# First projection reordered: queries, keys, values; second filters behind the queries; low parts and absolute sums on VectorE

## The chip, the cores and the metric

The kernel runs on one core of one Trainium2 chip. The metric is the device time of one execution in microseconds; of several executions the median is given. TensorE (PE) multiplies, VectorE (DVE), ScalarE (ACT) and GpSimd (POOL) work on elements, SyncE (SP) issues most transfers.

## What is computed

A two-layer backbone over 256 latent tokens of width 1024, with 256 context tokens. Layer 0 mixes by a Hyena long convolution and a neighbourhood attention from one combined projection; layer 1 by a Fourier transform; then a dense SwiGLU and a top-2-of-8 expert SwiGLU. The part around the change, cut from the reference:

```python
h  = modulate(rmsnorm(x, g_mix), sh1, sc1)          # 256 x 1024
z  = h @ w_in                                       # 3072 columns
q, k, v = split(z[..., 1536:], 3)                   # 512 each
hc = modulate(rmsnorm(ctx, g_mix), csh1, csc1)
kc, vc = split(hc @ w_in[:, 2048:], 2)              # context: keys and values only
y_na = neighborhood_attention(q, k, v, kc, vc, rpb)
filt = k / (sum(abs(k), axis=0) + EPS)              # two implicit filters, from a small sine network
y = x1 * long_conv(v_hy, filt[:, 0]);  y = x2 * long_conv(y, filt[:, 1])
x = x + gt1 * (concat([y_hy, y_na]) @ w_mix_out)
```

## The kernel before

All matrices are float32. A projection is made of three multiplications: each operand is split into a high part that the fast float format holds (ScalarE copies it) and a low part (the difference, an elementwise subtraction), and `mm3` (lines 105 to 108) issues high x low, low x high and high x high in turn.

Up to the output projection a scheduler orders the instructions; it takes the program's order as priority and places what it holds to be ready. The queues of PE, VectorE, ScalarE, GpSimd and SyncE each run strictly in the order it wrote.

- `ada_first` (line 117) multiplies the conditioning with the first ada weights, eight pieces of 1 MB (L130), and gives the scales a_x and a_c (line 204).
- `filters(o)` (line 362) makes filter o: four multiplications h2 x fw3 (L367) into psB buffers, each times a decay on VectorE (L369); the absolute values on ScalarE (L373); their sums on GpSimd (L374, L375) into absum; sum and difference of the two sides on VectorE (L377, L378). `spectra(o)` (line 381) multiplies these with a cosine and a sine table (L353) and adds and subtracts the halves (L343 to L348, into kre and kim). L460 adds absum over the partitions.
- `hT_split` (line 219) takes the normalised rows, transposes two 128-column blocks at a time on PE into a psA buffer (L224; there are two psA buffers), scales them into hf (one half on ScalarE, L228, one on VectorE, L229; two hf buffers), copies the high part on ScalarE (L233) and subtracts for the low part (L234). It is called for the latent rows (four pieces, hxh and hxl) and for the context rows (four pieces, hch and hcl). The low part is taken by VectorE, but GpSimd takes the first latent piece and all four context pieces.
- `proj` (line 411) splits 128 columns of the weights (L113 on ScalarE, L114 on VectorE, tiles wsh and wsl, two buffers) and multiplies them into a psA buffer: 24 multiplications for latent rows, 24 more for context rows if `both`. The loop at line 448 goes over six 1 MB pieces of w_in: 8 and 9 are keys, 10 and 11 values, 6 and 7 queries; each has two chunks, keys and values with context rows (48 multiplications), queries without (24). `qkv_chunk` (line 426) moves the result into qT, kT, vb and vc, the values with further transposes (L441, L445).
- `filters(1)` stands ahead of that loop, `spectra(1)` behind it. After the loop the context tiles are given back (`es_hc.close`) and their memory goes to attention.
- `dense` (line 536) lists the Hyena work: twelve chunks of 24 multiplications (`in_step`, z by L473 to L476) and the two convolutions; `issue` mixes them with 32 heads of attention (`Head`, lines 593 to 642): scores (L609 to L615, from qm, which ScalarE copies from qT at L571), maximum (L619), exp (L621), transposes (L626), values (L637, L640). The ada weights of later steps are added up on VectorE (L153).
- From the output projection on, the order is written by hand: the dense SwiGLU, the Fourier layer, the experts.

The lines that the change rewrites:

```python
374        nc.gpsimd.tensor_add(ab[0], ab[0], ab[1])
375        nc.gpsimd.tensor_add(absum[:, o, :], ab[0][:, 0, :], ab[0][:, 1, :])
404    hT_split(np_, xnx, a_x, b_x, hxh, hxl, 0, psA, "a", sub=lambda k: (nc.gpsimd, nc.vector)[k > 0])
407    hT_split(np_, xnc, a_c, b_c, hch, hcl, 0, psA, "a", sub=lambda k: nc.gpsimd)
408    with tc.issue_after(last_mm[0]):
409        filters(1)
448    for n in (8, 9, 10, 11, 6, 7):
452        if n == 7:
453            with tc.issue_after(last_mm[0]):
454                spectra(1)
```

Of the kernel before, what the change touches and what calls it, by code (L numbers as in the profile page):

```python
# [34 lines left out]
def backbone(ctx, tc, x, c, cx, c_ctx, w_ada, b_ada, norm_g, w_in, short_w, short_b,  # L35
# [4 lines left out]
    nc = tc.nc  # L40
# [62 lines left out]
    last_mm = [None]  # L103
# [115 lines left out]
    def hT_split(pool, xn, a, b, hi, lo, off, ps_pool, tag, keep=None, each=None, sub=None):  # L219
        for k2 in range(4):  # L220
            ps = T(ps_pool, [P, 2, 2 * P], tag)
            for kk in range(2):
                for t in range(2):
                    nc.tensor.transpose(ps[:, kk, t * P:(t + 1) * P],  # L224
                                        xn[:, t, (2 * k2 + kk) * P:(2 * k2 + kk + 1) * P], ident)
            hf = keep[:, 2 * k2:2 * k2 + 2, :] if keep is not None else T(pool, [P, 2, 2 * P], "hf", bufs=2)
            k = 2 * k2
            nc.scalar.activation(hf[:, 0, :], ps[:, 0, :], AF.Identity, bias=b[:, k:k + 1], scale=a[:, k:k + 1])  # L228
            nc.vector.tensor_scalar(hf[:, 1, :], ps[:, 1, :], a[:, k + 1:k + 2], b[:, k + 1:k + 2],  # L229
                                    op0=OP.mult, op1=OP.add)  # L230
            if hi is not None:
                hs = hi[:, k:k + 2, off:off + 2 * P]
                nc.scalar.copy(hs, hf)  # L233
                (sub or (lambda k: nc.vector))(k2).tensor_sub(lo[:, k:k + 2, off:off + 2 * P], hf, hs.bitcast(F32))  # L234
            if each is not None:
                each(k2)
# [11 lines left out]
    hxh = T(hx, [P, ND, S], "hxh", F32R)  # L248
# [113 lines left out]
    def filters(o):  # L362
        hr = T(fp, [P, 2, 2, 512], "hr")
        for t in range(2):
            for d in range(2):
                ps = T(psB, [P, 512], "b")
                nc.tensor.matmul(ps, h2[:, t * P:(t + 1) * P],  # L367
                                 fw3[:, (2 * o + d) * 512:(2 * o + d + 1) * 512], start=True, stop=True)
                nc.vector.tensor_mul(hr[:, t, d, :], ps, decay[:, t, :])  # L369
        nc.vector.memset(hr[0:1, 0, 1, :], 0.0)  # L370
        ab = [T(fp, [P, 2, 512], "ab", bufs=2) for _ in range(2)]
        for t in range(2):
            nc.scalar.activation(ab[t], hr[:, t], AF.Abs)  # L373
        nc.gpsimd.tensor_add(ab[0], ab[0], ab[1])  # L374
        nc.gpsimd.tensor_add(absum[:, o, :], ab[0][:, 0, :], ab[0][:, 1, :])  # L375
        hp = T(fp, [P, 2, 512], "ab", bufs=2)
        nc.vector.tensor_add(hp, hr[:, :, 0, :], hr[:, :, 1, :])  # L377
        nc.vector.tensor_sub(hr[:, :, 0, :], hr[:, :, 0, :], hr[:, :, 1, :])  # L378
        fbox[o] = (hp, hr)
# [21 lines left out]
    b_c = modx[:, 0:2, :].rearrange("p a b -> p (a b)")  # L401
    xnx = normalise(np_, x_sb, "nx")
    xnc = normalise(np_, ctx_box[0], "nc", out=ctx_box[0], junk=kim[:, 1].rearrange("p a b -> p (a b)"))
    hT_split(np_, xnx, a_x, b_x, hxh, hxl, 0, psA, "a", sub=lambda k: (nc.gpsimd, nc.vector)[k > 0])
    with tc.issue_after(last_mm[0]):
        spectra(0)
    hT_split(np_, xnc, a_c, b_c, hch, hcl, 0, psA, "a", sub=lambda k: nc.gpsimd)
    with tc.issue_after(last_mm[0]):
        filters(1)

    def proj(w, both, eng=None):
        wh, wl = split(wsp, w, [P, ND, P], "ws", eng=eng)
# [32 lines left out]
                nc.tensor.transpose(tp[:, t, :], vT[:, S + t * P:S + (t + 1) * P], ident)  # L445
            nc.vector.tensor_copy(vc[:, :, cs], tp[:, 0:2, :])

    for n in (8, 9, 10, 11, 6, 7):
        w = win_piece(n)
        for j in range(2):  # L450
            qkv_chunk(w[:, :, j * P:(j + 1) * P], 2 * n + j - 12)
        if n == 7:
            with tc.issue_after(last_mm[0]):
                spectra(1)
    es_hc.close()
    es_f.close()
    psn = T(psS, [P, 8], "s")
# [1272 lines left out]
```

## Time and profile before

| | |
|---|---|
| median of 3 runs | 1470.87 us (1466.68 to 1473.18) |
| profiled execution | 1472.97 us, its span 1471.1 us |
| mean granted clock of TensorE | 0.989 of full speed |
| PE busy | 1412.9 us (96%) |
| DVE, ACT, POOL busy | 587.3, 322.8, 115.5 us |
| HBM read | 465.48 MB, 317 GB/s over the span |

In a timeline row stand the start in us, the length in us, the engine, the line, the operation, the tiles out<-in (buffer numbers left out) with their forms, and how many instructions the row merges; in brackets the idle time of the engine just before it and what ended it. Instructions overlap a little: the price of one in a row of its kind is the distance from start to start.

### The profile page before, as it was taken

What the parts mean: (1) busy time and instruction counts of PE and PEld (TensorE: products, weight loads), DVE (VectorE), ACT (ScalarE), POOL (GpSimd) and SP (SyncE); (2) the same over time, 40 slices, a digit from 0 to 9 for tenths busy, and PEclk for the clock granted to TensorE, in tenths of its full rate; (3) what the DMA queues carried; (4) which work ended last, traced back from release to release, by engine and by line L of the source; (5) the groups of instructions that cost most, each with busy time, mean ns of one, the idle gap of its engine ahead of it and who ended that gap; (6) DMA issues with size and microseconds to landing.
All of it is one profiled execution on the core that took longest, in us unless ns stands there. A gap on an engine that the chain in (4) does not pass through costs nothing.

```text
span 1471.1 us, 23080 instructions
## 1 busy us (share of the span) xinstructions
PE 1412.9 (96%) x9597; PEld 768.6 (52%) x9597; DVE 587.3 (40%) x942; ACT 322.8 (22%) x613; POOL 115.5 (8%) x107
## 2 busy tenths in 40 slices
PE   6999999989999898999999999998999999999997
PEld 1598677779899764334335333333335333333332
DVE  3636888789999763102112110114212111012412
ACT  3425444554444441000001000000101010000001
POOL 1501110023351010000000000000000000000000
PEclk9999999999999999999999999999999999999999
DMA  9435454279999766999999999999899999999895
GB/s 350 135 92 160 158 187 171 87 278 372 330 321 337 260 237 234 367 378 363 387 396 388 395 393 393 394 393 391 317 395 387 394 393 393 394 394 388 316 393 226
DMA packets 205398, 468.42 MB, mean 318 GB/s; under 512 B 8559, under 2 KB 43728, under 8 KB 204168
## 3 DMA queue, kind: packets, MB, share of 16 engines
q1 hardware_dynamic: 202576, 462.03, 85.2%
q0 software_dynamic: 1680, 2.29, 0.7%
q10 hardware_dynamic: 1000, 2.24, 0.5%
q8 instruction: 85, 1.39, 0.4%
q14 instruction: 57, 0.47, 0.1%
HBM read 465.48 MB, written 1.05 MB: 317 GB/s over the span
## 4 chain that ended last, share of the span: by engine, by line
PE 60%; DVE 1%; issue 0%; ACT 0%
PE w L1518 27%; PE y L1550 13%; PE w L1514 9%; PE y L1543 4%; PE w L1531 2%; PE y L1258 1%; PE w L1580 1%; PE w L1258 1%; PE y L1580 1%; PE w L1573 1%; DVE ysb L1560 0%; DVE total L1582 0%; DVE aT L1535 0%; DVE ysb L1562 0%; DVE x L1664 0%
## 5 line engine op out<-in xcount | busy, mean ns | idle before, releaser
L1518 PE MATMUL w<-w,hg 128*64 128x512 f32 x1792 | 401.9, 597 | 2.7 <-issue 2.7
L1518 PEld LDWEIGHTS w<-w,hg 128*64 128x64 f32 x1792 | 124.1, 137 | 241.1 <-issue 237.2
L1550 PE MATMUL y<-w,aT 128*64 128x512 f32 x896 | 200.8, 595 | 1.5 <-DVE aT L1535 1.5
L1522 ACT ACTIVATE a<-w 64x512 f32<-64x512 f32 (+1 forms) x91 | 46.5, 511 | 661.7 <-PE w L1518 451.7
L1523 DVE TENSOR_TENSOR a<-a,w 64x512 f32<-64x512 f32 (+1 forms) x91 | 52.8, 580 | 327.7 <-ACT a L1522 327.7
L1535 DVE COPY aT<-w 128x256 f32<-128x256 f32 (+2 forms) x77 | 31.1, 411 | 311.8 <-PE w L1531 290.9
L1514 PE MATMUL w<-w,hg 128*32 128x256 f32 x2240 | 132.7, 381 | 0.0
L1550 PEld LDWEIGHTS y<-w,aT 128*64 128x64 f32 x896 | 61.9, 137 | 132.6 <-issue 129.8
L1514 PEld LDWEIGHTS w<-w,hg 128*32 128x32 f32 x2240 | 67.0, 109 | 64.1 <-issue 24.2
L106 PE MATMUL f<-hh,wh 128*128 128x256 f32 x344 | 97.3, 283 | 0.8 <-ACT hh L933 0.8
L108 PE MATMUL f<-hh,wl 128*128 128x256 f32 x344 | 96.7, 281 | 0.5 <-DVE wl L114 0.5
L107 PE MATMUL f<-hl,wh 128*128 128x256 f32 x344 | 96.6, 281 | 0.1
L113 ACT CAST wsh<-w 128x1024 fp32r<-128x1024 f32 x57 | 59.4, 1046 | 74.0 <-PE a L107 50.1
L114 DVE TENSOR_TENSOR wl<-w,wh 128x1024 fp32r<-128x1024 f32 x46 | 69.9, 1560 | 6.1 <-ACT wh L113 6.1
L1543 PE MATMUL y<-w,aT 128*32 128x512 f32 x560 | 66.8, 594 | 2.7 <-DVE aT L1535 2.7
L106 PEld LDWEIGHTS f<-hh,wh 128*128 128x128 f32 x344 | 64.8, 188 | 1.9 <-ACT hh L933 1.0
L107 PEld LDWEIGHTS f<-hl,wh 128*128 128x128 f32 x344 | 64.8, 188 | 1.3 <-DVE hl L934 0.3
L108 PEld LDWEIGHTS f<-hh,wl 128*128 128x128 f32 x344 | 64.8, 188 | 0.7 <-DVE wl L114 0.7
L114 DVE TENSOR_TENSOR wsl<-w,wsh 128x1024 fp32r<-128x1024 f32 x39 | 48.5, 1246 | 37.2 <-ACT wsh L113 37.0
L114 POOL TENSOR_TENSOR wsl<-w,wsh 128x1024 fp32r<-128x1024 f32 x18 | 52.1, 2893 | 118.3 <-ACT wsh L113 118.3
L106 PE MATMUL a<-hxh,wsh 128*128 128x256 f32 x192 | 54.9, 286 | 0.9 <-DVE z L476 0.9
L820 DVE SCALAR_TENSOR_TENSOR adacc<-w,colAs,adacc 128x1024 f32<-128x1024 f32 x32 | 55.4, 1733 | 0.3
(441 smaller groups left out, 1835.7 us busy)
## 6 DMA issues: line engine op xcount, KB each, us to landing
w<-in_moe_w_dram SPq DMA_DIRECT2D x336, 1024.0 KB
w<-in_w_ada_dram SPq DMA_DIRECT2D x44, 1024.0 KB
w<-in_ffn_w_dram SPq DMA_DIRECT2D x33, 1024.0 KB
w<-in_w_in_dram SPq DMA_DIRECT2D x12, 1024.0 KB
w<-in_w_mix_out_dram SPq DMA_DIRECT2D x4, 1024.0 KB
w<-in_w_fourier_dram SPq DMA_DIRECT2D x4, 1024.0 KB
s<-in_w_ada_dram SPq DMA_DIRECT2D x2, 1024.0 KB
raw<-in_na_rpb_dram POOLq DMA_DIRECT2D x32, 62.5 KB, 3.0
```

The lines of the kernel that those rows point to most:

```text
L106: nc.tensor.matmul(ps, lh, rh, start=first, stop=False)
L107: nc.tensor.matmul(ps, lh, rl, start=False, stop=False)
L108: last_mm[0] = nc.tensor.matmul(ps, ll, rh, start=False, stop=last).ins
L113: nc.scalar.copy(hi, src)
L114: (eng or nc.vector).tensor_sub(lo, src, hi.bitcast(F32))
L820: nc.vector.scalar_tensor_tensor(st["acc"], w, colA_s[:, k:k + 1], st["acc"], op0=OP.mult, op1=OP.add)
L1514: nc.tensor.matmul(ps[32 * j:32 * j + 32, 0:256], hg[:, k, 0:32], w, start=(k == 0), stop=(k == ND - 1), tile_position=(0, 32 * j))
L1518: nc.tensor.matmul(ps[64 * j:64 * j + 64, :], hg[:, k, 0:64], ws[j][k // 4][:, k % 4, :], start=(k == 0), stop=(k == ND - 1), tile_positio ...
L1522: nc.scalar.activation(a[b3:b3 + 64, 0:n], ps[b1:b1 + 64, 0:n], AF.Silu)
L1523: nc.vector.tensor_mul(a[b3:b3 + 64, 0:n], a[b3:b3 + 64, 0:n], ps[b3:b3 + 64, 0:n])
L1543: nc.tensor.matmul(y[32 * j:32 * j + 32, :], aT[:, f, 32 * q:32 * q + 32], w2[fc // 2][:, fc % 2, h * 512:(h + 1) * 512], start=(first and ...
L1550: nc.tensor.matmul(y[64 * j:64 * j + 64, :], aT[:, f, :], w2[f // 2][:, f % 2, h * 512:(h + 1) * 512], start=(first and f == 0), stop=(las ...
```

## The change

The first projection takes pieces 6 and 7 (queries) first, then 8 and 9 (keys), then 10 and 11 (values). `filters(1)` is called behind the last query chunk instead of ahead of the loop, `spectra(1)` behind the last value chunk. The low parts of all pieces of `hT_split` and the two additions of absolute values are VectorE's.

```diff
@@ filters @@
-        nc.gpsimd.tensor_add(ab[0], ab[0], ab[1])
-        nc.gpsimd.tensor_add(absum[:, o, :], ab[0][:, 0, :], ab[0][:, 1, :])
+        nc.vector.tensor_add(ab[0], ab[0], ab[1])
+        nc.vector.tensor_add(absum[:, o, :], ab[0][:, 0, :], ab[0][:, 1, :])
@@ backbone @@
-    hT_split(np_, xnx, a_x, b_x, hxh, hxl, 0, psA, "a", sub=lambda k: (nc.gpsimd, nc.vector)[k > 0])
+    hT_split(np_, xnx, a_x, b_x, hxh, hxl, 0, psA, "a")
     with tc.issue_after(last_mm[0]):
         spectra(0)
-    hT_split(np_, xnc, a_c, b_c, hch, hcl, 0, psA, "a", sub=lambda k: nc.gpsimd)
-    with tc.issue_after(last_mm[0]):
-        filters(1)
+    hT_split(np_, xnc, a_c, b_c, hch, hcl, 0, psA, "a")
...
-    for n in (8, 9, 10, 11, 6, 7):
+    for n in (6, 7, 8, 9, 10, 11):
         w = win_piece(n)
         for j in range(2):
             qkv_chunk(w[:, :, j * P:(j + 1) * P], 2 * n + j - 12)
-        if n == 7:
+        if n in (7, 11):
             with tc.issue_after(last_mm[0]):
-                spectra(1)
+                (filters if n == 7 else spectra)(1)
```

What the scheduler makes of it, at three places. PE's order around the context transposes (a_367 to a_397 are psA buffers with transposes of the context rows, w_240; b_... are psB buffers of the second filters), before:

```order
L353 MATMUL b_361<-hr_186,dft_113 128x512
L367 MATMUL b_408<-fw_32_140,fh_44_184 128x512
L224 MATMUL a_367<-ident_61,w_240 128x128 x4
L224 MATMUL a_377<-ident_61,w_240 128x128 x4
L367 MATMUL b_411<-fw_32_140,fh_44_184 128x512
L224 MATMUL a_387<-ident_61,w_240 128x128 x4
L367 MATMUL b_414<-fw_32_140,fh_44_184 128x512
L224 MATMUL a_397<-ident_61,w_240 128x128 x4
L367 MATMUL b_417<-fw_32_140,fh_44_184 128x512
L106 MATMUL a_436<-hxh_80,wsh_432 128x256
```

In the changed program the same place, and the place behind the fourth query chunk (a_505), ahead of the first key chunk (a_560):

```order
L353 MATMUL b_361<-hr_186,dft_113 128x512
L224 MATMUL a_367<-ident_61,w_240 128x128 x4
L224 MATMUL a_377<-ident_61,w_240 128x128 x4
L224 MATMUL a_387<-ident_61,w_240 128x128 x4
L224 MATMUL a_397<-ident_61,w_240 128x128 x4
L106 MATMUL a_413<-hxh_80,wsh_409 128x256
...
L108 MATMUL a_505<-hxh_80,wsl_502 128x256
L367 MATMUL b_532<-fw_32_140,fh_44_184 128x512
L367 MATMUL b_535<-fw_32_140,fh_44_184 128x512
L367 MATMUL b_538<-fw_32_140,fh_44_184 128x512
L106 MATMUL a_560<-hxh_80,wsh_556 128x256
```

The four L367 have left the transposes; three stand together behind the queries, the fourth eight multiplications later.

VectorE's order in the changed program from the scaling of the last two latent pieces to that of the third context piece (a_387); what stands ahead of it there are the scalings of the first two latent pieces and the two halves of kre:

```order
L234 TENSOR_TENSOR hxl_81<-hf_316,hxh_80 128x512
L234 TENSOR_TENSOR hxl_81<-hf_326,hxh_80 128x512
L114 TENSOR_TENSOR wsl_410<-w_407,wsh_409 128x1024
L229 TENSOR_SCALAR hf_336<-a_331,a_x_286,mod_8_74 128x256
L229 TENSOR_SCALAR hf_346<-a_341,a_x_286,mod_8_74 128x256
L344 TENSOR_TENSOR kim_118<-sE_359,b_361 128x512
...
L229 TENSOR_SCALAR hf_382<-a_377,a_c_288,modx_76 128x256
L114 TENSOR_TENSOR wsl_440<-w_407,wsh_439 128x1024
L234 TENSOR_TENSOR hcl_285<-hf_372,hch_284 128x512
L234 TENSOR_TENSOR hcl_285<-hf_382,hch_284 128x512
L229 TENSOR_SCALAR hf_392<-a_387,a_c_288,modx_76 128x256
```

Before, hxl of hf_316 and all four hcl were GpSimd's and stood nowhere in this row, the second wsl stood behind the last context piece, and two L369 stood between the scalings of the first three context pieces.

ScalarE's order where attention begins (z of the last Hyena chunks a_1399 and a_1451, qm, the first probabilities pe) in the changed program:

```order
L113 CAST wsh_1447<-w_1393 128x1024
L471 ACTIVATE z_1103<-a_1340,colA_71 128x256
L471 ACTIVATE z_1103<-a_1399,colA_71 128x256
L471 ACTIVATE z_1103<-a_1451,colA_71 128x256
L569 COPY qm_1123<-qT_90 32x128 x8
L619 ACT_TABLE_LOAD
L619 ACTIVATE pe_1277,sums_1133<-s_1271,nm_1134 128x384
```

Before, L571 (now L569) stood behind z of a_1241, the fourth Hyena chunk, and four chunks followed it. On PE the scores of the first head now stand behind the last multiplication of a_1451.

## Rows read from the trace of the kernel before

**Rows 1.** The page's slices: PE's busy tenths in 40 equal slices.
```profile
PE   6999999989999898999999999998999999999997
```
**Rows 2.** PE's timeline from 28 to 66 us.
```profile
40.93 1.05 PE L460 MATMUL s<-ones,absum 128*128 128x1 f32 x8 [0.95 <-POOL absum L375]
...
57.34 1.12 PE L367 MATMUL b<-fw,fh 64*128 64x512 f32 x2
58.39 0.66 PE L224 MATMUL a<-ident,w 128*128 128x128 f32 x4
58.98 1.12 PE L367 MATMUL b<-fw,fh 64*128 64x512 f32 x2
60.03 0.39 PE L106 MATMUL a<-hxh,wsh 128*128 128x256 f32 x1
```
**Rows 3.** PE's timeline: projection chunks at 72 to 84 us, Hyena chunks at 132 us.
```profile
72.31 0.39 PE L108 MATMUL a<-hxh,wsl 128*128 128x256 f32 x1 [0.35 <-DVE wsl L114]
...
77.83 0.28 PE L106 MATMUL a<-hxh,wsh 128*128 128x256 f32 x1
...
83.49 0.28 PE L106 MATMUL a<-hxh,wsh 128*128 128x256 f32 x1
...
132.64 0.35 PE L106 MATMUL a<-hxh,wsh 128*128 128x256 f32 x1 [0.46 <-DVE z L476]
```
**Rows 4.** VectorE's timeline from 38 to 54 us and at 149 us.
```profile
38.52 1.22 DVE L377 TENSOR_TENSOR ab<-hr 128x1024 f32<-128x1024 f32 x1 [2.24 <-POOL ab L374]
...
47.30 0.16 DVE L204 SCALAR_TENSOR_TENSOR a_c<-modx,colA 128x8 f32<-128x8 f32 x1
...
52.25 0.68 DVE L234 TENSOR_TENSOR hxl<-hf,hxh 128x512 fp32r<-128x512 f32 x1
52.85 0.53 DVE L229 TENSOR_SCALAR hf<-a,a_x,mod 128x256 f32<-128x256 f32 x1
53.30 0.67 DVE L344 TENSOR_TENSOR kim<-sE,b 128x512 f32<-128x512 f32 x1
...
149.38 1.28 DVE L153 SCALAR_TENSOR_TENSOR adacc<-w,colAs,adacc 128x1024 f32<-128x1024 f32 x1
```
**Rows 5.** Windows: PE, PEld, DVE, ACT, POOL busy (instructions), granted clock, DMA share, GB/s.
```profile
42.00:44.00 2.00, 2.00 (x12) 0.50 (x16) 0.00 (x0) 0.00 (x0) 0.00 (x0) 0.56 0.05 11
44.00:46.00 2.00, 2.00 (x10) 0.50 (x2) 0.67 (x1) 0.00 (x0) 0.00 (x0) 0.59 0.00 0
...
54.00:56.00 2.00, 1.06 (x6) 0.71 (x6) 2.00 (x4) 1.28 (x3) 0.00 (x0) 1.00 0.00 0
...
188.00:192.00 4.00, 2.64 (x17) 2.12 (x16) 4.00 (x7) 0.78 (x1) 0.00 (x0) 0.63 0.94 291
...
544.00:548.00 4.00, 2.28 (x13) 1.56 (x12) 2.35 (x6) 1.61 (x5) 1.13 (x2) 0.93 0.00 0
548.00:552.00 4.00, 4.00 (x36) 1.53 (x35) 1.13 (x2) 2.28 (x5) 3.19 (x4) 0.65 0.01 4
```
**Rows 6.** GpSimd's timeline at 57 us.
```profile
57.47 1.27 POOL L234 TENSOR_TENSOR hcl<-hf,hch 128x512 fp32r<-128x512 f32 x1 [6.23 <-ACT hch L233]
```
**Rows 7.** ScalarE's timeline from 139 to 146 us.
```profile
139.41 0.56 ACT L473 ACTIVATE z<-a,colA 128x256 f32<-128x256 f32 x1
139.87 2.46 ACT L571 COPY qm<-qT 32x128 f32<-32x128 f32 x8
...
144.61 1.28 ACT L621 ACT_TABLE_LOAD   x1
145.91 0.58 ACT L621 ACTIVATE pe<-s,nm 128x384 f32<-128x384 f32 x1
```
**Rows 8.** PE's timeline from 158 to 192 us.
```profile
158.00 0.59 PE L609 MATMUL s<-kT,qm 128*128 128x256 f32 x2
...
159.31 0.31 PE L637 MATMUL o<-vb,pT 128*64 128x32 f32 x4
...
190.72 0.80 PE L615 MATMUL s<-bias,jrev 128*128 128x128 f32 x2 [1.36 <-DVE bias L602]
```

## The prediction

> **What bounds the kernel now.** I read the slices of the page first. PE stands at 8 or 9 tenths from the second slice to the last [rows 1], so nothing but PE's own chain sets the end: a change pays if it takes a wait or a stretch of low clock out of PE's row, and costs if it puts one in. Everything the change touches lies in the first 210 us. I therefore went to PE's timeline from 28 to 66 us [rows 2], where the normalised rows are transposed and split and the second filters are multiplied. PE waits there for absum from GpSimd (0.95 us before L460) and for ScalarE and VectorE before the L367 multiplications. The first projection multiplication stands at 60.03; from there a chunk of 48 runs through in 5.66 us (77.83 to 83.49), so 24 of them take 2.83 us [rows 3]. VectorE's row shows what paces the transposes: from 48 us on one operation starts where the last ends (52.25, 52.85, 53.30 [rows 4]). Last I read the granted clock by stretch [rows 5]: it fell to half (1.2 GHz) for most of 42 to 46 us after the wait at L460, again in 188 to 192 us and after 544 to 548 us, where PE had been busy for 2.28 of 4 us, but not in 54 to 56 us, where it was busy for 1.06 of 2 us.
>
> **The change part by part.**
>
> *Sums of absolute values on VectorE.* The additions L374 and L375 leave GpSimd. On VectorE they are two additions of the forms that stand in [rows 4], 128x1024 at 1.22 us and 128x512 at 0.68 us, and they fall into the 2.24 us in which VectorE waits for GpSimd's sum ahead of L377. So absum is there before PE reaches L460, and the 0.95 us wait goes. **-0.95 us.**
>
> *First low parts on VectorE.* Five subtractions of 512 elements leave GpSimd, 1.27 us each there [rows 6], and cost VectorE 0.60 us each from start to start [rows 4]. What PE waits for is in the compiled order: the first projection chunk takes the psA buffer that the third context piece leaves, so it starts when VectorE has scaled that piece (L229 on a_387). Ahead of that, counted from a_c at 47.30, VectorE now has six L229 at 0.45, ten operations of 512 elements at 0.60 (kre, kim, six low parts) and two wsl of L377's size, 1.22: 2.7 + 6.0 + 2.4 = 11.1 us, with 0.7 us until its first L229 may start and 0.55 for the L229 itself and the hand-over, 12.4 us. In the kernel before it was 60.03 - 47.46 (end of a_c) = 12.57 us. **-0.2 us.** So VectorE's two added low parts, and one wsl that moved ahead, eat what the four L369 and the memset leave. Bounds: if the buffer did not gate, the last query low part would (four L229, seven of 512, one wsl, the same 0.7: 7.9 us), -4.5 us; if VectorE stands still once for ScalarE, a wsl's length, +1.2 us.
>
> The Trainium skill, "GPSIMD Engine Reference", section Engine selection, would have elementwise additions on VectorE because GpSimd is about twice as slow with two inputs. The rows agree on the price of one (1.27 against 0.68 us); by that rule five of them would bring the start forward by 5 x 0.6 = 3.0 us and the sum would be 2.8 us lower than mine. I don't take it, because here VectorE is the queue and GpSimd was not.
>
> *Second filters behind the queries.* The four L367 cost 1.05 us each from start to start (57.34 to 58.39 [rows 2]). Before, they stood in time in which PE waited for the transposes anyway, so their removal there gains nothing beyond the start above. Now three stand back to back behind the fourth query chunk and one eight multiplications later, in a row that has no waits: 4 x 1.05 = **+4.2 us**, between 3.4 (if a fifth of it is the change of operands, which goes where three stand together) and 4.5 (1.12 us, the length of one). VectorE's part (four L369, memset, the sums, L377, L378: some 8 us) lies beside a K chunk of 5.66 us and the next; wsl for the chunk after stands behind it and is needed only 5.66 us later. The wait of 0.35 us for wsl at 72.31 [rows 3], which had L378 ahead of it, goes: **-0.35 us.**
>
> *The clock at the first chunk.* Without the L367, PE has in the last 8 us ahead of the first chunk only four groups of transposes, 0.6 us each (58.39 to 58.98 [rows 2]): 2.4 us of work. That is thinner than 544 to 548 us, which was followed by half clock, but also than 54 to 56 us, which was not. I take one fall of the length of the one at 42 us (0.44 x 2 x 2 us + 0.41 x 2 x 2 us = 3.4 us at half speed [rows 5]), which costs half of that: **+1.7 us**, between 0 and 3.4.
>
> *Queries first.* Twelve chunks and their loads are the same in number. w_in pieces 6 and 7 are in before 50 us as 8 and 9 were; the third comes early into the buffer of the last ada weights, the fourth waits for the context transposes as before and is wanted 20 us later. No load is late: 0. What changes is what stands beside what. Before, the context tiles were free after the eight long chunks and attention could begin within the fifth hyena chunk; now they are free only when the hyena chunks begin. In the compiled order all eight hyena chunks stand ahead of the first scores. Two things follow.
>
> First, hyena chunks wait for VectorE's z on every second one (0.46 us at 132.64 [rows 3], and once more). With eight in a row instead of five, there are three such waits instead of two: **+0.46 us.**
>
> Second, attention starts bare. ScalarE copies z of the last chunk (0.46 from start to start), then the eight qm (2.46 us), then loads the exp table (1.28) and only then does the first exp (0.58), all in [rows 7]. PE has the scores of two heads to do, 1.31 us each (158.00 to 159.31 [rows 8]): it waits 0.9 us for the first qm, 0.2 for the bias, ends at 3.7 us, and gets the first probabilities at 5.0. **+2.4 us**, between 0.9 (if the copies were early) and 3.3. Before, a projection chunk covered all that. Behind that, four L153 (1.28 us each, as the one at 149.38 in [rows 4]) that stood beside hyena chunks now stand ahead of the convolution's products, and so do four heads of PE work, whose scores alone are 5.2 us. So the wait of PE for VectorE at 190.72 (1.36 us, [rows 8]) should rather shrink: **-0.4 us**, between -1.4 (gone) and +5.1 (the four L153 whole).
>
> Sum: -0.95 - 0.2 + 4.2 - 0.35 + 1.7 + 0.46 + 2.4 - 0.4 = **+6.9 us**. The profiled execution (1472.97 us) would become 1479.9. It stands 2.10 us above the median of the runs, so the median goes to 1470.87 + 6.9 = **1477.8 us**. All later stages keep their order and move as one.
>
> **The rivals.**
>
> *A, slower: the clock falls twice.* Attention's start has PE busy for 2.6 of its first 5 us, about as thin as 188 to 192 us (2.64 of 4 us, clock 0.63). If it falls there too, for 3.4 us, and the fall at the first chunk takes the double of that and costs 1.7 us more, 6.9 + 1.7 + 1.7 gives 10.3: 1481.2. It decides as soon as one of the two is added (+8.6). For it speak the stretches at 42, 188 and 544 us, against it 54 to 56 us.
>
> [...]
>
> *B, the clock helps instead.* The fall at 42 to 46 us followed the wait at L460, which goes. If it goes with it and the first chunk runs at full clock, 6.9 - 1.7 - 1.7 = +3.5: 1474.4. Against it: L460 itself, eight tiny multiplications in 1.05 us, stays.
>
> *C, faster: the queries do start early.* If the buffer does not gate (-4.5 us), the clock stays up at both places as in B (-3.4), and the wait at 190.72 us goes with the other order (-1.4) together with the half clock around it (0.37 x 2 x 4 = 3.0 us in 188 to 192 us, half of it lost, -1.5): 6.9 - 10.8 = -3.9, 1467.0. The compiled order speaks against it at the first step.
>
> **How the numbers follow.** My forecast 0.45, with its own range 1472 to 1482; A 0.28; B 0.15; C 0.12. A measurement of this kernel can tell about 0.5% (7.35 us) from no change. A third of my own case lies above +7.35 (0.15), with A that makes slower 0.43. Two thirds of my case (0.30), B (0.15) and half of C (0.06) make no difference, 0.51. The other half of C, where one more fall of the clock goes with the new order, is faster, 0.06. Range: 1466 (C and 1 us of scatter) to 1487 (A with the wait for the convolution at its upper bound, 1481.2 + 5.5), which leaves out some 0.15.
>
> **What would show it.** No wait at L460; the first projection multiplication 12 to 13 us behind a_c, at about 58.9; clock at half just before or in the first query chunk; four L367 of about 1 us behind the fourth query chunk with no wait around them; a gap of about 0.9 us ahead of the first scores and one over 1 us ahead of the first transposed probabilities. I am wrong if the first chunk starts before 56 us, if L367 costs PE nothing where it now stands, or if the first exp does not wait for its table.

## The result, and the profile after

The changed kernel takes 1480.5 us (median of 6 runs, 1478.5 to 1483.9) against 1467.9 us of the kernel before (6 runs, 1466.3 to 1473.2): 12.6 us slower by the medians; ratio 1.0074, 95% interval 1.0050 to 1.0099, which is some 10.9 us. Run once more, it took 1480.0 us (7 runs), ratio 1.0068 (1.0043 to 1.0093). The profiled executions lie closer, 1477.3 us of span against 1471.1, since the one of before was among the slower of its six runs; the second pair of profiles has 1480.0 against 1470.8. Two lines have gone, so L460 is now L458, L609 L607, and so on.

Where the time went is read by stages, from the start of the same instruction in four profiles (both kernels were profiled a second time, below):

| stage, us | before | before again | changed | changed again |
|---|---|---|---|---|
| to the end of a_c | 47.46 | 47.21 | 44.15 | 45.16 |
| a_c to the first projection multiplication | 12.57 | 12.56 | 12.31 | 12.33 |
| from there to the first transposes of z | 101.24 | 101.24 | 110.02 | 111.14 |
| z to the first out-projection multiplication | 107.85 | 107.70 | 110.98 | 109.39 |
| out-projection, to the first FFN multiplication | 33.53 | 33.54 | 33.54 | 33.54 |
| FFN to the end of the span | 1168.45 | 1168.55 | 1166.30 | 1168.44 |

2.0 to 3.3 us are gained ahead of a_c, 9 to 10 us lost in the projections and at the start of attention, and 1.5 to 3.3 us in the convolution.

PE's slices read much as in [rows 1]; the change cannot be seen there:

```profile
PE   6899899989999898999999999998999999999997
```

PE's timeline of the changed kernel, in the places of [rows 2] and [rows 3]:

```profile
39.21 1.05 PE L458 MATMUL s<-ones,absum 128*128 128x1 f32 x8
...
49.73 1.11 PE L224 MATMUL a<-ident,w 128*128 128x128 f32 x8 [1.67 <-DVE hf L229]
53.04 1.11 PE L224 MATMUL a<-ident,w 128*128 128x128 f32 x8 [2.20 <-DVE hf L229]
56.46 0.58 PE L106 MATMUL a<-hxh,wsh 128*128 128x256 f32 x1 [2.31 <-DVE hf L229]
...
60.47 0.42 PE L106 MATMUL a<-hxh,wsh 128*128 128x256 f32 x1
60.69 0.41 PE L107 MATMUL a<-hxl,wsh 128*128 128x256 f32 x1
...
61.36 0.28 PE L108 MATMUL a<-hxh,wsl 128*128 128x256 f32 x1
61.48 0.28 PE L106 MATMUL a<-hxh,wsh 128*128 128x256 f32 x1
...
70.05 3.03 PE L367 MATMUL b<-fw,fh 64*128 64x512 f32 x6
...
74.14 1.12 PE L367 MATMUL b<-fw,fh 64*128 64x512 f32 x2
```

The wait for absum has gone. Three waits for VectorE's scaling stand where the L367 were. The first query chunk starts at 0.21 us per multiplication and goes over to 0.12 us at 61 us. The L367 run back to back behind the fourth chunk. The granted clock of the same stretch (columns as in [rows 5]):

```profile
42.00:44.00 2.00, 2.00 (x15) 1.31 (x12) 1.01 (x5) 0.59 (x1) 0.05 (x1) 1.00 0.19 53
44.00:46.00 2.00, 2.00 (x9) 1.00 (x9) 1.45 (x5) 1.90 (x4) 2.00 (x4) 1.00 1.07 373
...
54.00:56.00 2.00, 0.15 (x2) 0.00 (x0) 1.91 (x4) 0.72 (x2) 0.00 (x0) 0.57 0.27 54
56.00:58.00 2.00, 1.54 (x7) 1.54 (x8) 1.61 (x3) 1.69 (x3) 0.00 (x0) 0.50 1.03 362
58.00:60.00 2.00, 2.00 (x11) 2.00 (x11) 0.69 (x1) 0.00 (x0) 0.00 (x0) 0.50 1.09 351
60.00:62.00 2.00, 2.00 (x15) 2.00 (x14) 0.00 (x0) 0.44 (x1) 0.00 (x0) 0.72 0.89 284
```

Half clock (1.2 GHz) at 42 to 46 us has gone; a longer stretch of it now begins at 54 us, behind 8 us in which PE was mostly waiting, and reaches into the first chunk. At attention's start (PE, where [rows 8] showed a covered one) and in the convolution:

```profile
153.43 0.70 PE L607 MATMUL s<-kT,qm 128*128 128x256 f32 x2 [0.83 <-ACT qm L569]
...
157.59 0.55 PE L624 MATMUL t<-ident,pe 128*128 128x128 f32 x3 [1.39 <-ACT pe L619]
...
186.68 0.49 PE L613 MATMUL s<-bias,jrev 128*128 128x128 f32 x2 [2.10 <-DVE bias L600]
```

The clock stayed up at attention's start:

```profile
154.00:158.00 4.00, 2.62 (x19) 1.63 (x19) 2.35 (x8) 3.91 (x11) 0.00 (x0) 1.00 0.00 0
158.00:162.00 4.00, 4.00 (x32) 2.63 (x30) 2.13 (x4) 1.63 (x6) 0.00 (x0) 1.00 0.00 0
```

### The profile page after: what moved, and what is told of

Same layout as the page of the kernel before. It is cut to its first block, busy times and chain, and to the rows that moved or that the text cites. A ratio compares the mean times of both kernels' runs of the same rounds, so it can differ in the third digit from the quotient of the medians.

```text
span 1477.3 us, 23084 instructions
## 1 busy us (share of the span) xinstructions
PE 1411.2 (96%) x9597; PEld 773.5 (52%) x9597; DVE 590.1 (40%) x951; ACT 323.5 (22%) x613; POOL 99.4 (7%) x98
## 3 DMA queue, kind: packets, MB, share of 16 engines
q8 instruction: 85, 1.39, 0.4%
HBM read 465.48 MB, written 1.05 MB: 316 GB/s over the span
## 4 chain that ended last, share of the span: by engine, by line
PE 59%; DVE 2%; issue 0%; ACT 0%
PE w L1516 26%; PE y L1548 13%; PE w L1512 8%; PE y L1541 4%; PE w L1529 2%; PE y L1256 1%; PE w L1578 1%; PE w L1256 1%; PE y L1578 1%; PE w L1571 0%; DVE ysb L1558 0%; DVE total L1580 0%; DVE aT L1533 0%; DVE ysb L1560 0%; DVE hg L1264 0%
## 5 line engine op out<-in xcount | busy, mean ns | idle before, releaser
L114 DVE TENSOR_TENSOR wl<-w,wh 128x1024 fp32r<-128x1024 f32 x46 | 69.8, 1559 | 6.0 <-ACT wh L113 6.0
L114 DVE TENSOR_TENSOR wsl<-w,wsh 128x1024 fp32r<-128x1024 f32 x39 | 47.6, 1222 | 46.2 <-ACT wsh L113 46.0
L114 POOL TENSOR_TENSOR wsl<-w,wsh 128x1024 fp32r<-128x1024 f32 x18 | 52.5, 2917 | 119.8 <-ACT wsh L113 119.8
L108 PE MATMUL a<-hxh,wsl 128*128 128x256 f32 x192 | 55.9, 291 | 0.0
```

The source lines that it names most:

```text
L108: last_mm[0] = nc.tensor.matmul(ps, ll, rh, start=False, stop=last).ins
L114: (eng or nc.vector).tensor_sub(lo, src, hi.bitcast(F32))
```

## The experiments

Two measures stand beside the median. The first is the start of the first out-projection multiplication in the profile, behind which nothing was changed. The second is the median of each run's time less (1 - its mean granted clock) x its span, called "less clock": an upper bound of what half clock took is taken off, and a kernel's runs then scatter less (before: 1464.6 to 1480.7 us as timed in the first set of runs, 1451.5 to 1459.4 so). Since it is an upper bound, a kernel with much half clock may come out too low by it. Differences of medians are taken across sets of runs; the ratio compares each kernel with before in its own set.

| kernel | median, us | ratio to before, 95% | less clock | out-projection at |
|---|---|---|---|---|
| before, beside four sets of runs | 1469.1 to 1470.2 | 1 | 1454.2 to 1456.4 | 269.1 |
| changed | 1480.5 | 1.0074 (1.0050 to 1.0099) | 1463.4 | 277.5 |
| again | 1471.2 | 0.9987 (0.9965 to 1.0009) | 1455.3 | 268.7 |
| sums | 1468.3 | 0.9983 (0.9960 to 1.0006) | 1452.5 | 265.7 |
| vec | 1469.0 | 0.9991 (0.9975 to 1.0007) | 1452.2 | 270.3 |
| order | 1480.7 | 1.0071 (1.0052 to 1.0091) | 1463.2 | 280.3 |
| ordsums | 1476.6 | 1.0043 (1.0021 to 1.0064) | 1458.1 | 278.8 |
| vecorder | 1478.8 | 1.0078 (1.0047 to 1.0109) | 1461.8 | 272.1 |
| ordfilt | 1483.7 | 1.0094 (1.0064 to 1.0124) | 1461.5 | 275.3 |
| earlyatt | 1477.4 | 1.0056 (1.0036 to 1.0077) | 1453.8 | 277.4 |
| ordearly | 1473.3 | 1.0038 (1.0021 to 1.0055) | 1453.8 | 276.1 |
| lateatt | 1471.6 | 1.0025 (1.0010 to 1.0041) | 1455.3 | 267.7 |
| afterwarm | 1483.1 | 1.0105 (1.0086 to 1.0124) | 1468.2 | 276.7 |
| changed again | 1480.0 | 1.0068 (1.0043 to 1.0093) | 1462.8 | 278.0 |

**The kernel before once more** (again; no edit).

> The kernel before, once more, unchanged. It tells how far two profiled executions of one program lie apart. The profile of before (1472.97 us) stands 5 us above the median of its six timed runs; the changed kernel's profile does not. Theory 1: the 5 us are stretches of half clock behind 496 us, which differ from execution to execution; then this profile shows other stretches there, the same waits up to 300 us, and a first out-projection multiplication at 269 us again, within 1 us. Rival: the fall of the clock at 42 to 46 us is itself one of those that come and go; then it is missing here and everything behind stands 2 to 3 us earlier.

The same waits, the same half clock at 42 to 46 us (0.59 in the four), out-projection at 268.7, and nearly the same stretches behind 496 us. So the theory that these explain the profile's 5 us was wrong: with more runs the median of before is 1469 to 1470, and its profile is an ordinary one. The rival fell too: the half clock at 42 us was there again.

**Sums on VectorE alone** (sums).

```diff
-        nc.gpsimd.tensor_add(ab[0], ab[0], ab[1])
-        nc.gpsimd.tensor_add(absum[:, o, :], ab[0][:, 0, :], ab[0][:, 1, :])
+        nc.vector.tensor_add(ab[0], ab[0], ab[1])
+        nc.vector.tensor_add(absum[:, o, :], ab[0][:, 0, :], ab[0][:, 1, :])
```

> The kernel before with the absolute sums on VectorE and nothing else. Theory 1 (the wait at the small multiplications was worth more than its 0.95 us, since the half clock of 42 to 46 us hung on it): no wait there, granted clock 1.00 in 42 to 46 us, a_c at 44.1 instead of 47.3 us, first projection multiplication 12.5 us behind it, at 56.7 instead of 60.0; total 3.0 to 3.5 us below before. Rival 2 (the price as forecast): wait gone, half clock still there, 0.9 us below before. Rival 3 (VectorE, which is the queue of the transposes, only waits later): the first projection multiplication still at 59 to 60 us, no difference.

PE's timeline and two windows of this kernel:

```profile
40.06 1.05 PE L460 MATMUL s<-ones,absum 128*128 128x1 f32 x8
...
57.56 0.39 PE L106 MATMUL a<-hxh,wsh 128*128 128x256 f32 x1
```
```profile
42.00:44.00 2.00, 2.00 (x15) 0.52 (x8) 0.69 (x1) 0.00 (x0) 0.00 (x0) 1.00 0.00 0
44.00:46.00 2.00, 2.00 (x12) 1.34 (x11) 0.92 (x5) 1.65 (x4) 0.00 (x0) 1.00 0.86 257
```

Theory 1 in the trace: no wait, full clock, first multiplication 2.5 us earlier than [rows 2] show, out-projection 3.4 us earlier. The timed runs put it 1.9 us below before, with no change inside the interval. Its median is the lowest in the table, by too little to be called faster. That the half clock hung on the wait alone does not hold everywhere, though: the kernel with the order and the filters (below) keeps the wait and has no half clock behind it.

**Sums and low parts on VectorE, order as before** (vec). The edit above, and

```diff
-    hT_split(np_, xnx, a_x, b_x, hxh, hxl, 0, psA, "a", sub=lambda k: (nc.gpsimd, nc.vector)[k > 0])
+    hT_split(np_, xnx, a_x, b_x, hxh, hxl, 0, psA, "a")
...
-    hT_split(np_, xnc, a_c, b_c, hch, hcl, 0, psA, "a", sub=lambda k: nc.gpsimd)
+    hT_split(np_, xnc, a_c, b_c, hch, hcl, 0, psA, "a")
```

> The kernel before with all of the change's moves to VectorE (sums and low parts), its order of chunks and its second filters where they were. Theory 1 (low parts move from an engine that was not the bottleneck to one that is): like the kernel with the sums alone, first projection multiplication 12 to 13 us behind a_c; total 2 to 4 us below before. Rival 2 (an elementwise operation saved on GpSimd is time saved): up to 3 us further down than the sums alone, 6 to 6.5 us below before. Rival 3 (VectorE's five additions of 0.6 us lengthen the queue): 3 us later than the sums alone, no difference to before.

PE's timeline of this kernel:

```profile
49.51 1.12 PE L367 MATMUL b<-fw,fh 64*128 64x512 f32 x2 [1.42 <-ACT sE L343]
50.56 1.83 PE L224 MATMUL a<-ident,w 128*128 128x128 f32 x8
...
56.51 3.78 PE L367 MATMUL b<-fw,fh 64*128 64x512 f32 x4
60.22 0.58 PE L106 MATMUL a<-hxh,wsh 128*128 128x256 f32 x1
```

In this profile the clock fell right behind the longer wait (0.50 from 52 us to beyond 62 us), and the first chunk starts 16 us behind a_c instead of 12.6. Yet the timed runs stand 0.7 us above the sums alone and 1.2 us below before: nearest to theory 1 by the times (it wanted 2 to 4 us), rival 3 by this one profile. That five subtractions saved on GpSimd are time saved (rival 2) is excluded: 6 us below before would be 0.9959.

**The order alone** (order), filters among the transposes, engines as before.

```diff
-    for n in (8, 9, 10, 11, 6, 7):
+    for n in (6, 7, 8, 9, 10, 11):
...
-        if n == 7:
+        if n == 11:
             with tc.issue_after(last_mm[0]):
                 spectra(1)
```

> The kernel before with queries, keys, values and the second filters among the context transposes as before; engines as before. Everything up to the last of the twelve chunks then stands as in before (first out of the way: last chunk ends within 1 us of before's). Theory 1 (attention starts bare behind all eight Hyena chunks): third wait for z (0.46), 0.8 us ahead of the first scores, 1.4 us ahead of the first transposed probabilities, then waits of PE for bias and pT of 1 to 3 us more in the convolution: first out-projection multiplication 4 to 6 us later than before's, total 4 to 6 us above before. Rival 2 (the order is free, and what the change lost it lost by the second filters and the clock at the first chunk): within 1 us of before.

It loses 10.5 us, as much as the changed kernel, but not at the same places. Half of it came where neither theory had put anything: with the new order the second group of small multiplications was compiled into the second query chunk.

```profile
69.95 1.05 PE L460 MATMUL s<-ones,absum 128*128 128x1 f32 x8 [2.79 <-POOL absum L375]
```
```profile
72.00:74.00 2.00, 2.00 (x14) 2.00 (x13) 1.53 (x4) 0.00 (x0) 2.00 (x5) 0.59 0.62 128
74.00:76.00 2.00, 2.00 (x12) 2.00 (x12) 0.06 (x1) 1.14 (x2) 1.07 (x2) 0.56 0.78 45
...
162.00:166.00 4.00, 4.00 (x23) 2.38 (x23) 1.95 (x3) 1.37 (x4) 0.00 (x0) 0.69 0.00 0
```

A wait of 2.8 us for GpSimd, half clock behind it, then the bare start of attention as forecast (0.83 and 1.38 us), and half clock behind that too, which the changed kernel did not have there.

**The order with the sums on VectorE** (ordsums; both edits).

> Queries, keys, values in that order and the absolute sums on VectorE; low parts and second filters as before. The kernel with the order alone stood 10.4 us (medians) above before; its trace shows 5 us of that in the second query chunk, where the second group of small multiplications now stood and waited 2.8 us for GpSimd's sum, and 5 us at the start of attention. Theory 1 (half of the order's cost is GpSimd's late sum in its new place, and VectorE's sum takes it away): no wait at the small multiplications in either place, first projection multiplication at 57.5 us, first out-projection multiplication at 269 - 3.4 + 0.5 + 2.2 + 1 to 3 = 269.5 to 271.5 us; total 0 to 3 us above before. Rival 2 (attention's bare start carries all of it): 7 to 8 us above before, like the order alone less the 2.5 us of the sums.

Rival 2 by the medians (7.2 us above before; 6.3 by the ratio), though attention's start does not carry all of it. The wait at the small multiplications has gone and with it 4.1 us of the order's cost. This profile has half clock from 52 to 66 us, with the rows of PE up to the first chunk in the same sequence as in the kernel with the sums alone, which had none:

```profile
54.00:58.00 4.00, 4.00 (x8) 1.21 (x6) 2.26 (x4) 2.37 (x5) 1.94 (x2) 0.50 0.01 2
58.00:62.00 4.00, 4.00 (x11) 2.15 (x11) 2.54 (x5) 2.12 (x4) 2.50 (x3) 0.50 0.42 114
62.00:66.00 4.00, 4.00 (x21) 4.00 (x20) 2.83 (x2) 0.96 (x1) 4.00 (x8) 0.52 0.77 233
```

**The change without the move of the filters** (vecorder; both moves to VectorE and the order).

> The whole change except that the second filters stay among the context transposes. Theory 1 (terms of the traces add up): against the order with VectorE sums, the low parts on VectorE cost what they cost in before's order (first projection multiplication 3 us later, at 60 us, with half clock before it): 3 to 5 us above that kernel, 3 to 8 us above before. The filters behind the queries then cost the changed kernel 4 us and give back about as much by an earlier first chunk. Rival 2 (the filters behind the queries are what loses): this kernel stands at before, the changed kernel 10 us above it. Rival 3 (they hide what they should): this kernel is 3 us or more slower than the changed one.

Rival 2 falls: 9.4 us above before, within 2 us of the changed kernel. So by the timed runs the move of the filters costs about nothing in sum. Theory 1 missed too: 9.4 us instead of 3 to 8, and the first projection multiplication, at 58.3 us, came 12.8 us behind a_c and at full clock. Of the 4.0 us that the filters cost behind the queries (below) the rows show only a part given back: this kernel has 0.59 and 0.43 us of waits for wsl, and its first chunk starts 0.5 us later behind a_c than the changed kernel's, with waits of 1.42 and 0.96 us ahead of L367. Its profile has the first out-projection multiplication at 272.1 us, 5.3 and 5.9 us earlier than the two of the changed kernel; that the timed runs don't show this gain is not explained. Against the order with the sums, the low parts on VectorE cost 2.2 us by the medians and 3.7 us less clock, but the intervals of the ratios overlap, and the profiles go the other way up to the out-projection (272.1 against 278.8; 3.5 us of that lie ahead of the first chunk, where the other kernel had half clock).

**The order and the filters, without the moves to VectorE** (ordfilt).

```diff
-    with tc.issue_after(last_mm[0]):
-        filters(1)
...
+        if n in (7, 11):
+            with tc.issue_after(last_mm[0]):
+                (filters if n == 7 else spectra)(1)
```

> The changed kernel's order and its second filters behind the queries, with sums and low parts left on GpSimd. Theory 1: the four filter multiplications cost 4.0 us behind the fourth query chunk and the thin stretch before the first chunk 2 us of clock; the wait at the first small multiplications and the half clock at 42 us stay; the second group of small multiplications stands behind the values again, without a wait; attention 2.7 us plus 1 to 3: 9 to 12 us above before, the same as order alone and as the changed kernel. Rival 2 (the moves to VectorE are what makes the new order bearable): 13 us or more above before.

14 us above before by six runs that spread over 10 us (less clock 6.6 us). The interval takes in theory 1's 9 to 12 us as well as rival 2's 13 or more: not settled. The first chunk came 12.7 us behind a_c, so VectorE's row paces it with or without GpSimd's help. One thing that theory 1 took for granted failed: the wait at the small multiplications stayed, longer than in before (1.43 against 0.95 us), but no half clock followed it, and a_c ended at 44.08 us as in the changed kernel (44.15):

```profile
39.19 1.05 PE L458 MATMUL s<-ones,absum 128*128 128x1 f32 x8 [1.43 <-POOL absum L375]
```
```profile
38.00:42.00 4.00, 2.81 (x24) 1.39 (x24) 2.19 (x2) 0.00 (x0) 1.14 (x1) 1.00 0.88 279
42.00:46.00 4.00, 4.00 (x22) 2.38 (x19) 2.51 (x8) 2.54 (x5) 0.00 (x0) 1.00 0.68 207
```

PE had reached this place 2.2 us earlier than in before (the L130 just ahead of the wait start at 36.70 instead of 38.91 us). So what the sums seem to gain ahead of a_c came here without them.

**The changed kernel with attention let in among the Hyena chunks** (earlyatt).

```diff
-        short_conv(proj(w, False), m)
+        with (tc.issue_after(last_s[0]) if 4 <= m < 8 and last_s[0] is not None else ExitStack()):
+            short_conv(proj(w, False), m)
...
-            nc.tensor.matmul(ps[:, 0:P], jrev, ...
+            last_s[0] = nc.tensor.matmul(ps[:, 0:P], jrev, ...).ins
```

> The changed kernel with one thing more: the Hyena chunks from the fifth on are held behind the first scores on PE, so that qm, the exp table and the first heads stand among them, as in before. Theory 1 (attention's bare start is 2.2 us of waits, a third wait for z 0.5, and what follows in the convolution, 2 to 3 us): no wait for qm or for the first exp, first out-projection multiplication 273 to 275 instead of 277.5 us; 3 to 5 us below the changed kernel, 6 to 8 us above before. Rival 2 (PE has the same work, and VectorE's adacc and bias in front of the convolution set its start anyway): the waits move to bias and pT, within 1 us of the changed kernel.

By time it is 2.6 to 3.1 us below the changed kernel (medians; the intervals overlap). Less clock it is 9 us below, with ranges that don't meet (1452.4 to 1454.7 against 1461.0 to 1464.6): back at before. The mean granted clock is 0.984 instead of 0.988, though, which is some 6 us. By the profile it is rival 2: the first out-projection multiplication stands at 277.4 us (277.5 and 278.0 in the changed kernel), where theory 1 wanted 273 to 275. Not settled. Two waits for z have gone, but the hold is paid for by a bare wait for qm and one for the bias, 2.3 us together against 2.2 us of waits in the changed kernel:

```profile
143.08 0.70 PE L609 MATMUL s<-kT,qm 128*128 128x256 f32 x2 [1.67 <-ACT qm L571]
...
144.81 0.49 PE L615 MATMUL s<-bias,jrev 128*128 128x128 f32 x2 [0.67 <-DVE bias L602]
```
```profile
142.00:146.00 4.00, 2.25 (x13) 1.68 (x14) 3.38 (x8) 3.87 (x11) 0.00 (x0) 0.91 0.28 57
146.00:150.00 4.00, 4.00 (x23) 3.69 (x22) 0.10 (x1) 1.55 (x4) 0.00 (x0) 0.67 0.51 205
```

**The order with the sums, and the same hold** (ordearly).

> Queries, keys, values, the absolute sums on VectorE, filters and low parts as before, and the Hyena chunks from the fifth on held behind the first scores. The same kernel without that hold stood 7 us (medians) above before, the one with the old order and the sums 1 to 2 us below it. Theory 1 (what the order costs, once GpSimd's late sum is out of it, is attention's start behind all eight Hyena chunks): no bare wait for the exp table, the time returns to that of the old order with the sums, 1467 to 1471 us, and with the granted clock's share taken off (one minus the mean granted clock, times the span) to 1452 to 1455. Rival 2 (the order has another cost, or the clock takes the gain back as it did in the changed kernel with the same hold): 1473 to 1477 us.

1473.3 us, rival 2: 3.3 us below the same kernel without the hold by the medians, 0.7 us by the ratios, and 4.3 us less clock. What still stands above the kernel with the sums alone looks like clock for the most part: 5.0 us by the medians (8.1 by the ratios), 1.3 us less clock.

**The opposite: the old order with the sums, attention held back** (lateatt).

```diff
+    while issued[0] < 8:
+        dense[issued[0]]()
+        issued[0] += 1
...
-            heads[n - 1].scores()
+            with (tc.issue_after(last_mm[0]) if n == 1 else ExitStack()):
+                heads[n - 1].scores()
```

> The opposite: keys, values, queries as before, sums on VectorE, and the first scores held behind all eight Hyena chunks; qm may be copied early here. If theory 1 (attention's bare start is what the order costs) holds, the kernel loses here what the order lost: a third wait for z (0.46 us), the exp table bare (1.4 us), longer waits for pT and bias in the convolution; first out-projection multiplication 3 to 5 us later than in the kernel with the sums alone (265.7 us), total 4 to 7 us above it, 1472 to 1475 us. Rival 2 (another cost of the order): within 2 us of the kernel with the sums alone.

3.3 us above the sums alone, and slower than before (1.0010 to 1.0041). With qm copied early only 0.20 us of the wait for the exp stayed bare:

```profile
150.09 0.55 PE L626 MATMUL t<-ident,pe 128*128 128x128 f32 x3 [0.20 <-ACT pe L621]
```

The third wait for z came (0.46), and 1.4 us more behind the transposes of z (a wait of 1.33 us for yal, 0.62 for pT). So holding attention back costs time in the old order too, and more than its first wait shows. Theory 1, with less than it expected by the medians and in the profile (3.3 us for 4 to 7, 6.2 by the ratios; out-projection 2.0 us later for 3 to 5).

**The changed kernel with PE kept busy among the transposes** (afterwarm).

```diff
+    def warm(k2):
+        ps = T(psO, [P, 256], "o")
+        for _ in range((0, 3, 4, 4)[k2]):
+            nc.tensor.matmul(ps, dft[:, 0, 0, :], decay[:, 0, 0:256], start=True, stop=True)
```

> The changed kernel with eleven multiplications of 128x256 (nothing reads them) behind the second, third and fourth context transposes, where PE waits 1.7, 2.2 and 2.3 us. Theory 1 (the half clock of 54 to 62 us comes from those waits and costs 2.2 us): granted clock 1.00 through the first query chunk, first projection multiplication still 12 to 13 us behind a_c, its multiplications 0.118 us apart from the first on; 2 us below the changed kernel, and a higher mean granted clock in the timed runs (0.988 there). Rival 2 (the clock falls for another reason, or later instead): half clock there or within the next chunks, within 1 us of the changed kernel.

The mechanism is borne out, by one profile, and the sum is not. Granted clock in the stretch where the changed kernel had half:

```profile
54.00:56.00 2.00, 2.00 (x12) 1.82 (x13) 2.00 (x4) 1.07 (x2) 0.00 (x0) 1.00 0.00 0
56.00:58.00 2.00, 2.00 (x13) 1.77 (x12) 1.52 (x4) 1.45 (x3) 0.00 (x0) 1.00 0.60 164
58.00:60.00 2.00, 2.00 (x18) 1.95 (x17) 1.61 (x3) 0.81 (x2) 0.00 (x0) 1.00 1.12 374
```

The first projection multiplication came 13.1 us behind a_c, 0.8 us later than without the added ones, and from a_c to the transposes of z it takes 121.2 us instead of 122.3 and 123.5. But the whole kernel is 3 us slower than the changed one. Behind 303 us its PE stands 4.0 us in waits called "issue" (2.8 of it at a line that had none in the changed kernel, whose sum is 1.1), far from any edit. What sets them is open.

**The changed kernel once more** (no edit).

> The changed kernel once more, unchanged, for a second profile and more timed runs. Theory 1 (the half clock at the first chunk and the bare start of attention belong to this program): half clock again between 53 and 62 us, first projection multiplication 12 to 13 us behind a_c, waits of 0.8 and 1.4 us at attention's start, first out-projection multiplication at 276 to 279 us; median 1479 to 1482 us, 10 to 12 us above before. Rival 2 (the half clock at the first chunk comes and goes, as it did in kernels with the same PE row before it): clock 1.00 there, and the first out-projection multiplication 2 to 3 us earlier.

Theory 1: half clock from 53 to 63 us, the same three waits (the last 1.46 us), 0.83 and 1.38 us at attention's start, the same median.

## Why the prediction came out right, point by point

I gave 1477.8 us, 1466 to 1487; measured were 1480.5 and 1480.0. As a difference the forecast was less good: +6.9 us against 10.9 by the ratio and 12.6 by the medians. That the time came closer is luck: I started from the median of three runs of before, 1470.87 us, and that of six is 3 us lower. The mechanisms of the first 160 us were right, two terms were badly sized with opposite signs, so that their errors partly cancel, and one sentence was wrong.

- **Sums on VectorE, -0.95.** Too small. The end of a_c moved by 2.0 to 3.3 us; by 2.5 in the kernel with the sums alone. I counted the wait at L460 and left the half clock behind it (1.7 us by [rows 5]) to rival B, holding that eight tiny multiplications in 1.05 us would bring it on anyway. They stayed and the half clock went. That it went because of the sums is not shown: it went as well in the kernel with the order and the filters, whose wait stayed.
- **Start of the first chunk, 12.4 us behind a_c.** 12.31 and 12.33. VectorE's queue was counted rightly; the low parts brought nothing there. The Trainium skill, "GPSIMD Engine Reference", section Engine selection, would have them on VectorE; priced by the rows, an estimate, that was 3 us. These runs show no such gain: sums and low parts together were no faster than the sums alone, and with the new order 2.2 us slower by the medians.
- **Four L367 exposed, +4.2.** (73.00 - 70.05) + (75.20 - 74.14) = 4.0 us, from the starts of the multiplications behind them. The wait of 0.35 us for wsl of [rows 3] went, as forecast.
- **Clock at the first chunk, +1.7.** 21 multiplications at 0.214 instead of 0.118 us: 2.0 us, in the second profile some 2.7 (its four query chunks took 0.64 us longer). That the thin stretch is the cause is shown as far as one profile goes: with multiplications in the waits the clock stays up. The Trainium skill, "TensorE: Matmul & The Clock Gate", section HAM oscillation, tells of a kernel whose groups of multiplications stood apart by waits for DMA, longer than these, and where each next group began at the low clock. The traces have the fall behind shorter waits too, here (1.46 to 2.31 us, with transposes between) and behind 72 us in the kernel with the order alone, but not at attention's start in either profile of the changed kernel (1.00 from 150 to 162 us).
- **A third wait for z, +0.46; attention bare, +2.4.** 0.46 us; 0.83 + 1.39 = 2.2 us of waits. Letting attention in or holding it back moved the medians by about 3 us in three pairs of kernels; by intervals only the last pair is apart. The terms from the first chunk to this place add up to 8.3 and 9.0 us (0.35 us for wsl taken off), and the stage grew by 8.8 and 9.9 us.
- **Wait for the convolution, -0.4.** Wrong in sign, and the step that failed: "so the wait of PE for VectorE at 190.72 should rather shrink". It grew from 1.36 to 2.10 us, waits for pT and pe from 1.20 to 2.25 us (0.39 and three of 0.62), and the stage by 1.5 to 3.3 us. In sum the waits are some 2 us longer. Half clock took at most 6.8 us from this stage in both profiles of before, 8.5 and 6.8 us in those of the changed kernel ((1 - granted clock) x 4 us, added over the windows of 4 us), which is why its first profile lost more. The heads that I counted as cover were used up first: VectorE had five L153 (6.4 us) between z's transposes and the products where before it had three, and the next three biases stood behind five products (VectorE's rows below) where before they stood behind two (at 176.13 us), so PE ran out of heads. This is read from the rows; no run tried it by itself.

```profile
185.20 1.22 DVE L510 TENSOR_TENSOR C<-C,E 128x1024 f32<-128x1024 f32 x1
186.34 0.69 DVE L600 TENSOR_TENSOR bias<-raw,mask 128x128 f32<-128x128 f32 x3
```

- **"All later stages keep their order and move as one."** They keep their order. They don't move as one: from the FFN on the changed kernel took 2.2 us less than before in its first profile and 0.1 us less in its second. A wait of 1.9 us came in (last section), and a wait called "issue" in the experts fell from 2.7 and 2.8 to 1.1 us.

To the first out-projection multiplication I had +6.9, and the profiles show +8.3 and +9.3. Rival A's 1481.2 is the nearest number, but its second fall of the clock, at attention's start, did not come.

Of the parts, the order carries most of the loss: +10.5 us by itself, +8.2 us by the medians on top of the sums. That it alone equals the changed kernel is chance, since half of its own loss was a wait for GpSimd's sum and the half clock behind it, which the changed kernel doesn't have. The sums gain 2 us at most. The filters' move is about even by the times, and some 5 us worse by the profiles up to the out-projection.

## What to carry to other kernels

A wait of PE can be worth itself and a stretch of half clock behind it; read the granted clock behind each wait before pricing its removal, in more than one kernel, since the wait for absum had half clock behind it in three profiles and none in a fourth. When work is moved, ask what it had been covering: here the queries had covered attention's start, and the filters had kept PE busy among the transposes. Where single executions scatter by 1%, compare the start of the first untouched instruction and the time less the clock's share beside the medians.

## What was not expected of the hardware

**A collision some 200 us behind the change.** In the FFN of the changed kernel VectorE's L982 takes 2.58 us instead of 0.42, since GpSimd's L114 begins just ahead of it; PE waits 1.93 us. VectorE, GpSimd and PE of the changed kernel:

```profile
360.24 2.58 DVE L982 TENSOR_TENSOR asl<-a,ash 128x256 fp32r<-128x256 f32 x1
```
```profile
359.33 3.21 POOL L114 TENSOR_TENSOR wsl<-w,wsh 128x1024 fp32r<-128x1024 f32 x1 [1.42 <-ACT wsh L113]
```
```profile
362.88 0.50 PE L108 MATMUL y<-wsh,asl 128*128 128x512 f32 x1 [1.93 <-DVE asl L982]
```

The same two operations in the kernel before, VectorE and GpSimd:

```profile
352.28 0.42 DVE L984 TENSOR_TENSOR asl<-a,ash 128x256 fp32r<-128x256 f32 x1
352.61 4.60 DVE L114 TENSOR_TENSOR wl<-w,wh 128x1024 fp32r<-128x1024 f32 x2
```
```profile
353.20 2.92 POOL L114 TENSOR_TENSOR wsl<-w,wsh 128x1024 fp32r<-128x1024 f32 x1 [4.78 <-ACT wsh L113]
```

There GpSimd begins 0.9 us behind, and it is VectorE's next operation (L114 in the second row), which PE does not wait for, that is stretched. Both profiles of the changed kernel have this wait, and so have the kernel without the filters' move and the one with the added multiplications; the other ten profiles don't. The Trainium skill, "SBUF — State Buffer", section Who interferes with whom, says that a VectorE instruction with two inputs in SBUF and a GpSimd instruction that reads SBUF exclude each other; these rows agree. Counted from the first FFN multiplication, GpSimd's operation begins at 48.3 us in the changed kernel and at 50.6 in the one before, and the FFN weight ahead of it came some 0.9 us later (ScalarE waits 2.36 instead of 1.46 us for its DMA). Why is open.

**The clock does not follow PE's rows alone.** With PE's rows up to the first chunk in the same sequence, the clock stayed up there in two kernels (sums, lateatt) and was at half for some 14 us, into the first chunk, in two (ordsums, ordearly). And it falls without a wait: in the changed kernel PE was busy all the time when the clock went to half, from 252 to 262 us:

```profile
250.00:254.00 4.00, 4.00 (x27) 2.80 (x26) 4.00 (x6) 3.17 (x11) 0.00 (x0) 0.78 0.60 240
254.00:258.00 4.00, 4.00 (x21) 3.21 (x21) 2.78 (x7) 0.90 (x3) 0.00 (x0) 0.50 0.00 0
258.00:262.00 4.00, 4.00 (x18) 3.02 (x18) 3.07 (x8) 0.48 (x1) 0.00 (x0) 0.50 0.00 0
```

What decides it between equal rows was not found.
